# A second place for the tokens of the residual stream, with loads one tile ahead

## The chip, the cores and the metric

The kernel runs on one core of one Trainium2 chip, in one launch. The metric is the device time in microseconds (us). A core has five engines that run their own instruction streams in order and wait for one another by semaphores: TensorE (PE: matrix products and transposes), VectorE (DVE), ScalarE (ACT), GpSimd (POOL) and SyncE (SP, which issues most DMAs). ScalarE issues DMAs too, on a queue of its own. In the profile PEld is TensorE's loading of weights, which overlaps its products.

## The reference

One inference step of an encoder with one layer, over 1024 prompt tokens and 32 sample tokens (1056 in all), 1024 wide, in float32:

```
h = rmsnorm(x);  z = h @ w_in + b_in
x += w_out @ concat[ mLSTM(4 heads) | stick-breaking attention(6 heads) | S5 state space ]
x += CrossAttn(rmsnorm(x), memory K/V)    # 4 heads, 256 memory tokens
x += ConvFFN(rmsnorm(x))                  # gated, causal convolution of width 3
y  = rmsnorm(x)
```

The outputs are y, the attention's keys and values, the states of the mLSTM, of the state space and of the convolution, and the keys and values of the memory.

## The kernel before, in words

Activations lie transposed, features on the 128 partitions and tokens along the free dimension. Each float32 operand of a large product is split into a rounded part and a rest (`w_hi`, `w_lo`; `hi`, `lo`), and a product is done as three: hi x hi, hi x lo, lo x hi. Tokens are treated in three thirds of 352 (`CW`), numbered c = 0, 1, 2, or in tiles of 128 (eight prompt tiles and one of 32 sample tokens).

After the input projection three parts run side by side on all engines: the stick-breaking attention, the state space part and the mLSTM in nine chunks, in the order 0, 1, 2, 8, 3, 4, 5, 6, 7 (chunk 8 is the sample). Their results go to DRAM: `d_ya` (mLSTM), `d_yb` (attention), `d_yc` (state space). While the mLSTM goes on, the main line projects the memory's keys and values (`dense(...)` with `ev_kv`, weights `in_w_xk` and `in_w_xv`, results stored to `d_mk`, `d_mv`), and then comes the output projection `w_out(c)`. It needs the mixer outputs of third c (`y_load`) and the residual stream `xT` (zone zx) of all tokens. `ev_res` adds each product to `xT`.

`load_xT` fills `xT`: it loads a tile of tokens, [128 tokens x 1024] floats, on ScalarE's queue into a ring named "xt2", transposes it on TensorE in two halves of four transposes (`tp`), and ScalarE copies each half into `xT`. The ring has one place, at the upper end of zone zg. `Window(..., 1)` lets one tile run at a time, and `w_out` waits until `xt_done` has nine entries (line 1882).

An mLSTM chunk loads five inputs: queries (`d_qa`), keys (`d_ka`), values (`d_va`), output gates (`d_oa`) and a row broadcast `d_uu`. GpSimd adds a mask to the last, ScalarE takes four exponentials of it, one for each head, and TensorE uses them in products (`gp`). The inputs' rings have three places; `refill` (lines 1218 to 1222) gives them a fourth once the attention is done (`stick_done`).

Memory: fixed zones are dealt out by `Mem`, the first free stretch that fits, in the order of the zones; `fits(n, kind)` asks whether there is one, `Bag` holds named rings, and `grow` adds a place to a ring. The zones of float32 are named zf, zy, zx, zg in the profile, those of rounded numbers zr, za, zb, zm. A stretch that was freed is written again only once its readers are done, and those waits come from its former use.

The order of the work is fixed in two steps. All operations pass through one helper (line 173, hence "L173" in every row). A planner with a clock for each engine decides in which order the parts emit their instructions: `add` puts a part at the side, `advance` lets the parts at the side run when their clock says that they are due, `until` turns the clock on until a condition holds. A scheduler then orders each engine's stream by a timeline of its own and inserts the waits. A change of one part's memory or cost therefore moves instructions of the others.

Of the kernel before, what the change touches and what calls it, by code (L numbers as in the profile page):

```python
# [15 lines left out]
P = 128  # L16
D = 1024
KD = D // P
T = 1024
TS = 32  # L20
# [33 lines left out]
def tile_fn(tc, *args):  # L54
    nc = tc.nc
    a = dict(zip(_INS, args[: len(_INS)]))
# [120 lines left out]
    s = Timed(nc.scalar, "act")  # L177
# [51 lines left out]
    def add(x, at=None, slack=0.0):  # L229
        sd = x if isinstance(x, Window) else Side(x, chain[0], slack)  # L230
        sides.insert(len(sides) if at is None else at, sd)
        return sd
# [28 lines left out]
    with ExitStack() as top:  # L261
# [31 lines left out]
        def fits(n, kind):  # L293
            return any(m >= n for z in zones[kind] for _, m in z.heap)
# [82 lines left out]
        def rot(pool, shape, tag, bufs, dt=F32):  # L377
            x = pool.tile(shape, dt, name=tag, tag=tag)
            turn[tag] = (turn.get(tag, -1) + 1) % bufs
            alias[x.name] = f"{tag}{turn[tag]}"  # L380
            return x
# [4 lines left out]
        def tp():  # L386
            return rot(pst, [P, 4, P], "tp", 3)


        class WStream:  # L390
# [6 lines left out]
            def load(self, most=1):  # L397
                i = self.at + len(self.ready) + len(self.raw)
                if len(self.raw) > most or i >= self.end:
                    return False  # L400
                ap, kt, cols, bufs, _ = self.src[i]
                raw = bufs()[0] if bufs else rot(wpool, [P, KD, P], "w_raw", 2)
                if isinstance(ap, list):
                    g.memset(raw[:, :kt, :cols], 0.0)
                    for c0, part in ap:
                        sy.dma_start(raw[:, :kt, c0:c0 + part.shape[1]], part.rearrange("(k p) n -> p k n", p=P))
                else:
                    sy.dma_start(raw[:, :kt, :cols], ap.rearrange("(k p) n -> p k n", p=P))
                self.raw.append(raw)
                return True  # L410
# [546 lines left out]
        stick_done = []  # L957
# [793 lines left out]

        def load_xT():
            ring = Bag({"xt2": (1, D)}, top=True)

            def one(i):
                n = P if i < 8 else TS
                xt = ring.tile([P, D], "xt2")
                s.dma_start(xt[:n], a["x_prompt"][0, i * P:(i + 1) * P, :] if i < 8 else a["x_sample"][0])
                yield
                for q in range(2):  # L1760
                    ps = tp()
                    for j in range(4):
                        k = 4 * q + j
                        pe.transpose(ps[:, j, :n], xt[:n, k * P:(k + 1) * P], ident[:n, :n])
                    s.activation(xT[:, 4 * q:4 * q + 4, i * P:i * P + n], ps[:, :, :n], AF.Copy)
                    yield
                xt_done.append(i)

            w = add(Window((one(i) for i in range(9)), 1))
            while not w.done:  # L1770
                yield
            ring.free()
# [30 lines left out]
        def y_first():  # L1803
            while not (stick_done and s5_done and {0, 1, 2} <= ml_done):
                yield
            yield from y_load(0)

        add(load_xT())
        add(y_first())
        mm_mov = lambda k, c: (m_hl[:, 0, k], m_hl[:, 1, k])  # L1810
# [745 lines left out]
```

## Time and profile before

| | |
|---|---|
| median of the runs (lowest to highest, 3 runs) | 1707.65 us (1707.08 to 1707.72) |
| the profiled execution: time | 1706.09 us |
| its span, first to last instruction | 1704.3 us |
| mean granted clock of TensorE | 0.989 |
| TensorE busy | 1635.9 us, 96% |
| VectorE, ScalarE, GpSimd busy | 1132.0, 754.4, 456.8 us |
| DMA | 229.91 MB, mean 135 GB/s |

The profiled execution is one run with a time of its own; the span lies within it. Busy time is time in which an engine works on an instruction. A row of a timeline says in square brackets how long the engine was idle before it and which engine's instruction, or which DMA, ended that; the names are those of the tile written and of the tile read. The stretch in which `load_xT` runs is 466 to 642 us.

### The profile page before, as it was taken

The page shows a single profiled execution, that of the slowest core. Times are in us where ns is not written, and L with a number is a line of the kernel's source. Part 1 is how long each engine was busy: PE and PEld are TensorE (multiplying, and loading weights), DVE is VectorE, ACT ScalarE, POOL GpSimd, SP SyncE. Part 2 cuts the span into 40 slices and gives each one's busy share as a digit, 9 for nine tenths or more (in the row PEclk, how much of TensorE's full clock was granted, in tenths as well). Part 3 has the DMA queues.
Part 4 walks back from the last instruction along what each step waited for, and adds up shares of the span by engine and source line. Part 5 has one row for each costly group of instructions (what it writes and reads, how often), then busy time and mean ns, then how long its engine had stood idle before and what let it go on. Part 6 is the DMA issues. An engine that isn't in the chain of part 4 may idle for free.

```text
span 1704.3 us, 30437 instructions
## 1 busy us (share of the span) xinstructions
PE 1635.9 (96%) x11616; PEld 1593.0 (93%) x11616; DVE 1132.0 (66%) x2213; ACT 754.4 (44%) x1480; POOL 456.8 (27%) x620
## 2 busy tenths in 40 slices
PE   6999999999999989999999989999999999999997
PEld 5989989999888889999999889999999999999997
DVE  6778878835796757766656788777777777333232
ACT  6434434545565644544444553444444445111143
POOL 4234335011214322200202546533333330000022
PEclk9999999999899999999999999999999999999999
DMA  7464544254479965456554555322222227332111
GB/s 217 145 168 113 137 110 106 78 160 134 118 227 255 284 200 156 133 164 182 171 168 123 166 171 155 99 83 86 76 76 76 76 63 254 115 100 76 47 66 66
DMA packets 331592, 229.91 MB, mean 135 GB/s; under 512 B 45612, under 2 KB 312907, under 8 KB 331191
## 3 DMA queue, kind: packets, MB, share of 16 engines
q1 hardware_dynamic: 311751, 211.86, 42.5%
q10 hardware_dynamic: 19696, 16.11, 3.2%
q8 instruction: 92, 1.51, 0.4%
q14 instruction: 53, 0.43, 0.1%
HBM read 170.95 MB, written 56.38 MB: 133 GB/s over the span
## 4 chain that ended last, share of the span: by engine, by line
PE 77%; DVE 8%; DMA 7%; ACT 2%; issue 2%; POOL 2%; SPq 0%; ACTq 0%; DVEq 0%; POOLq 0%
PE mm L173 47%; PE gp L173 19%; PE tp L173 11%; DVE zy L173 3%; DVE zf L173 2%; DVE zr L173 1%; DVE zx L173 1%; POOL zy L173 1%; DMA zf<-d_act 1%; DMA out_dram<-zf 1%; POOL zf L173 1%; DVE w_lo L173 1%; ACT zf L173 1%; ACT zy L173 1%; DMA w_raw<-in_w_out_dram 1%
## 5 line engine op out<-in xcount | busy, mean ns | idle before, releaser
L173 PE MATMUL mm<-zb,w_hi 128*128 128x352 f32 (+4 forms) x1234 | 360.7, 329 | 2.9 <-ACT zb L173 1.2
L173 PE MATMUL mm<-zr,w_hi 128*128 128x352 f32 (+2 forms) x1358 | 282.2, 311 | 8.6 <-DVE zr L173 3.7
L173 PE MATMUL mm<-zb,w_lo 128*128 128x384 f32 (+4 forms) x858 | 283.6, 331 | 0.0
L173 POOL TENSOR_TENSOR zf<-zf 128x352 f32<-128x352 f32 (+5 forms) x98 | 117.5, 1200 | 579.9 <-ACT zf L173 500.5
L173 ACT ACTIVATE w_hi<-w_raw 128x1024 fp32r<-128x1024 f32 (+1 forms) x150 | 149.5, 997 | 275.0 <-PE mm L173 194.7
L173 PEld LDWEIGHTS mm<-zb,w_hi 128*128 128x128 f32 x1234 | 226.2, 190 | 4.7 <-ACT zf L173 1.3
L173 PE MATMUL mm<-zr,w_lo 128*128 128x264 f32 (+2 forms) x1026 | 225.6, 303 | 1.4 <-ACT zf L173 0.7
L173 PEld LDWEIGHTS mm<-zr,w_hi 128*128 128x128 f32 x1358 | 213.5, 189 | 10.3 <-DVE zr L173 3.9
L173 DVE TENSOR_TENSOR w_lo<-w_raw,w_hi 128x1024 fp32r<-128x1024 f32 (+1 forms) x127 | 159.9, 1259 | 60.5 <-ACT w_hi L173 59.9
L173 PE MATMUL mm<-za,w_hi 128*128 128x384 f32 (+1 forms) x552 | 184.2, 334 | 0.5 <-DVE za L173 0.5
L173 DVE TENSOR_TENSOR zx<-mm,zx 128x352 f32<-128x352 f32 (+3 forms) x120 | 62.7, 523 | 169.1 <-PE mm L173 168.7
L173 PEld LDWEIGHTS mm<-zb,w_lo 128*128 128x128 f32 x858 | 163.4, 190 | 0.7
L173 PEld LDWEIGHTS mm<-zr,w_lo 128*128 128x128 f32 x1026 | 158.6, 189 | 2.1 <-DVE w_lo L173 1.2
L173 PE MATMUL mm<-zy,w_hi 128*128 128x352 f32 x456 | 113.1, 324 | 0.0
L173 PE MATMUL tp<-ident,zf 128*128 128x128 f32 (+4 forms) x534 | 89.3, 285 | 24.6 <-DVE zf L173 21.7
L173 PE MATMUL gp<-zy 128*128 128x132 f32 (+12 forms) x698 | 105.7, 289 | 2.8 <-issue 2.1
L173 ACT ACTIVATE zf<-gp 128x512 f32<-128x512 f32 (+6 forms) x180 | 75.6, 476 | 73.6 <-PE gp L173 58.6
L173 DVE TENSOR_TENSOR zy<-zy 128x16 f32<-128x16 f32 (+9 forms) x370 | 98.5, 308 | 14.0 <-POOL zy L173 5.5
L173 PEld LDWEIGHTS mm<-za,w_hi 128*128 128x128 f32 x552 | 106.0, 192 | 1.2 <-DVE za L173 0.6
L173 POOL TENSOR_TENSOR zy<-zy 128x16 f32<-128x16 f32 (+8 forms) x123 | 83.0, 687 | 70.3 <-DVE zy L173 55.8
L173 PEld LDWEIGHTS gp<-zy 128*128 128x128 f32 (+4 forms) x698 | 93.7, 184 | 4.9 <-issue 2.9
L173 PEld LDWEIGHTS tp<-ident,zf 128*128 128x128 f32 (+4 forms) x534 | 65.0, 146 | 34.2 <-DVE zf L173 20.2
(241 smaller groups left out, 3354.3 us busy)
## 6 DMA issues: line engine op xcount, KB each, us to landing
w_raw<-in_w_ffn_a_dram SPq DMA_DIRECT2D x27, 512.0 KB
w_raw<-in_w_out_dram SPq DMA_DIRECT2D x24, 512.0 KB
w_raw<-in_w_xq_dram SPq DMA_DIRECT2D x24, 512.0 KB
w_raw<-in_w_xo_dram SPq DMA_DIRECT2D x24, 512.0 KB
w_raw<-in_w_in_dram SPq DMA_DIRECT2D x23, 512.0 KB
d_act<-zx SPq DMA_DIRECT2D x22, 528.0 KB
zf<-d_act SPq DMA_DIRECT2D x22, 528.0 KB
w_raw<-in_w_ffn_down_dram SPq DMA_DIRECT2D x16, 512.0 KB
```

The source lines that it names most:

```text
L173: return f(*args, **kw)
```

## The change

The load becomes a function of its own. It is called once at the start and again after the second half of each tile has been copied out. When a tile begins, the attention is done, the ring has one place and 1024 floats fit somewhere, the ring gets a second place and one load more is issued at once. The place is found by `Mem` as any other, here the first that fits in zone zf, and is used until all nine tiles are through.

```diff
--- before.py
+++ after.py
@@ -1751,11 +1751,24 @@
 
         def load_xT():
             ring = Bag({"xt2": (1, D)}, top=True)
+            came = []
+
+            def load():
+                i = len(came)
+                if i < 9:
+                    n = P if i < 8 else TS
+                    came.append(ring.tile([P, D], "xt2"))
+                    s.dma_start(came[i][:n], a["x_prompt"][0, i * P:(i + 1) * P, :] if i < 8 else a["x_sample"][0])
+
+            load()
 
             def one(i):
                 n = P if i < 8 else TS
-                xt = ring.tile([P, D], "xt2")
-                s.dma_start(xt[:n], a["x_prompt"][0, i * P:(i + 1) * P, :] if i < 8 else a["x_sample"][0])
+                xt = came[i]
+                if stick_done and len(ring.ring["xt2"][0]) == 1 and fits(D, "F"):
+
+                    ring.grow("xt2", D)
+                    load()
                 yield
                 for q in range(2):
                     ps = tp()
@@ -1763,6 +1776,8 @@
                         k = 4 * q + j
                         pe.transpose(ps[:, j, :n], xt[:n, k * P:(k + 1) * P], ident[:n, :n])
                     s.activation(xT[:, 4 * q:4 * q + 4, i * P:i * P + n], ps[:, :, :n], AF.Copy)
+                    if q:
+                        load()
                     yield
                 xt_done.append(i)
```

The first place at which the order changes for the argument is ScalarE around 520 us. `zf<-zf,zy` are the four exponentials of mLSTM chunk 5, `zy<-zy 32x32` those of chunk 8, `zf<-mm` and `zr<-mm` evacuate a product of the memory's keys. Before:

```order
L173 ACT_TABLE_LOAD
L173 ACTIVATE zf_87<-zf_87,zy_91 128x128 [waits Pool_49]
L173 ACTIVATE zf_87<-zf_87,zy_91 128x128 [waits DVE_49]
L173 ACTIVATE zf_87<-zf_87,zy_91 128x128 x2
L173 ACTIVATE zy_91<-zg_5311 128x96 [waits DVE_49]
L173 ACTIVATE zy_91<-zg_5311 128x96 x3
L173 ACTIVATE zx_5303<-tp_5846 128x4x128 [waits PE_49]
L173 ACTIVATE zf_87<-mm_5813 128x256 [waits DMAHW3_49,PE_49]
L173 ACTIVATE zr_83<-mm_5813 128x256 [waits DMAHW0_49]
L173 ACTIVATE zy_91<-zy_91 32x32 [waits DMAHW3_49,Activation_49,Pool_49]
L173 ACTIVATE zy_91<-zy_91 32x32 [waits Activation_49] x2
```

After:

```order
L173 ACTIVATE zf_87<-mm_5814 128x256 [waits DMAHW2_49,DVE_49,PE_49]
L173 ACTIVATE zr_83<-mm_5814 128x256 [waits DMAHW7_49]
L173 ACTIVATE zy_91<-zg_5311 128x96 [waits DVE_49]
L173 ACTIVATE zy_91<-zg_5311 128x96 x3
L173 ACTIVATE w_hi_5963<-w_raw_5812 128x1024 [waits DMAHW6_49,PE_49]
L173 ACTIVATE zf_87<-mm_5894 128x256 [waits DMAHW2_49,PE_49]
L173 ACTIVATE zr_83<-mm_5894 128x256 [waits DMAHW3_49]
L173 ACT_TABLE_LOAD [waits DMAHW1_49,Activation_49]
L173 ACTIVATE zy_91<-zy_91 32x32 [waits Pool_49]
L173 ACTIVATE zy_91<-zy_91 32x32 [waits Activation_49] x2
L173 ACTIVATE zy_91<-zy_91 32x32
```

Chunk 5's exponentials are gone from here (its `d_uu` is loaded later, into zy), and chunk 8's stand behind a further evacuation.

The second is ScalarE around 545 us in before's trace. `zf<-mm` evacuates the first product of the memory's values (mm_6024 before, mm_6057 after); `zy<-zy 128x128` are exponentials, of chunk 3 before, of chunk 4 after, and `128x96` rows are squares of a chunk's outputs. Before:

```order
L173 ACTIVATE zg_5311<-tp_6064 128x384 [waits PE_49]
L173 ACTIVATE zy_91<-zy_91 128x128 [waits DMAHW6_49,Pool_49]
L173 ACTIVATE zy_91<-zy_91 128x128 x3
L173 ACTIVATE zx_5303<-tp_6076 128x4x128 [waits PE_49]
L173 ACTIVATE zf_87<-mm_6024 128x256 [waits PE_49,Activation_49]
L173 ACTIVATE zr_83<-zf_87 128x1056 [waits DMAHW2_49]
L173 ACTIVATE zx_5303<-tp_6105 128x4x128 [waits PE_49]
L173 DMA zg_5311<-in_x_prompt_dram 128x1024 [waits DMAHW4_49,DMAHW1_49]
```

After:

```order
L173 ACTIVATE zy_91<-zy_91 32x96 [waits DVE_49]
L173 ACTIVATE zy_91<-zy_91 32x96 x3
L173 ACTIVATE zy_91<-zg_5311 128x96 [waits DVE_49,PE_49,Activation_49]
L173 ACTIVATE zy_91<-zg_5311 128x96 [waits PE_49,Activation_49] x3
L173 ACTIVATE zy_91<-zy_91 128x128 [waits DMAHW1_49,Pool_49]
L173 ACTIVATE zy_91<-zy_91 128x128 x2
L173 ACTIVATE zf_87<-mm_6057 128x256 [waits DMAHW4_49]
L173 ACTIVATE zy_91<-zy_91 128x128
L173 ACTIVATE zr_83<-tp_6113 128x256 [waits DMAHW3_49,DVE_49]
```

The evacuation stood behind chunk 3's exponentials; it now stands behind chunk 3's squares and two of chunk 4's exponentials, and the values' transposes (tp_6113) wait for it.

The third is TensorE near the end of the first third's output projection. mm_7073 is its last group, mm_7162 the first of the second third; `tp<-ident,zg 128x128` transposes the eighth tile of tokens, `tp<-ident,zf 128x32` that of the sample. Before:

```order
L173 MATMUL mm_7073<-zr_83,w_hi_7033 128x352 x2
L173 MATMUL mm_7073<-zr_83,w_lo_7034 128x352
L173 MATMUL mm_7073<-zr_83,w_hi_7033 128x352 x2
L173 MATMUL tp_6805<-ident_122,zg_5311 128x128 [waits DMAHW1_49,PE_49]
L173 MATMUL tp_6805<-ident_122,zg_5311 128x128 x3
L173 MATMUL tp_6811<-ident_122,zg_5311 128x128 [waits PE_49]
L173 MATMUL tp_6811<-ident_122,zg_5311 128x128 x3
L173 MATMUL mm_7073<-zr_83,w_lo_7034 128x352
L173 MATMUL mm_7162<-zr_83,w_hi_7067 128x352 [waits DVE_49,Activation_49]
L173 MATMUL mm_7162<-zr_83,w_hi_7067 128x352 [waits DVE_49]
L173 MATMUL mm_7162<-zr_83,w_lo_7068 128x352
```

After:

```order
L173 MATMUL mm_7039<-zr_83,w_hi_6999 128x352 x2
L173 MATMUL mm_7039<-zr_83,w_lo_7000 128x352
L173 MATMUL mm_7073<-zr_83,w_hi_7033 128x352 [waits DVE_49,Activation_49]
L173 MATMUL mm_7073<-zr_83,w_hi_7033 128x352
L173 MATMUL tp_6818<-ident_122,zf_87 128x32 [waits DMAHW0_49,PE_49]
L173 MATMUL tp_6818<-ident_122,zf_87 128x32 x3
L173 MATMUL tp_6824<-ident_122,zf_87 128x32 [waits PE_49]
L173 MATMUL tp_6824<-ident_122,zf_87 128x32 x3
L173 MATMUL mm_7073<-zr_83,w_lo_7034 128x352 [waits DVE_49]
L173 MATMUL mm_7073<-zr_83,w_hi_7033 128x352 x2
L173 MATMUL mm_7073<-zr_83,w_lo_7034 128x352
```

Before, the eighth tile's transposes stood at the end of mm_7073, and the sample's inside the next third. After, the eighth tile has been transposed before, and the sample's transposes stand at the start of mm_7073.

## Rows read from the trace of the kernel before

**Rows 1.** The page: busy us, share of the span, instructions of each engine.

```profile
PE 1635.9 (96%) x11616; PEld 1593.0 (93%) x11616; DVE 1132.0 (66%) x2213; ACT 754.4 (44%) x1480; POOL 456.8 (27%) x620
```

**Rows 2.** Windows: stretch, length, busy us (count) PE PEld DVE ACT POOL, clock, DMA share, GB/s.

```profile
500.00:520.00 20.00, 20.00 (x183) 19.88 (x182) 17.16 (x38) 12.10 (x28) 4.70 (x7) 1.00 0.96 268
520.00:540.00 20.00, 17.96 (x149) 17.49 (x148) 12.82 (x26) 12.88 (x44) 10.92 (x10) 0.91 0.82 218
540.00:560.00 20.00, 16.40 (x142) 15.17 (x141) 13.02 (x24) 10.49 (x28) 8.40 (x9) 1.00 1.05 290
...
580.00:600.00 20.00, 20.00 (x171) 19.98 (x170) 15.31 (x34) 12.85 (x43) 4.86 (x6) 1.00 0.91 273
...
620.00:640.00 20.00, 13.84 (x76) 13.11 (x75) 9.03 (x9) 8.20 (x12) 4.27 (x3) 0.83 0.90 263
640.00:660.00 20.00, 20.00 (x135) 19.92 (x134) 17.02 (x28) 11.68 (x18) 0.96 (x2) 1.00 0.61 183
```

**Rows 3.** DMA issues, 500 to 642 us: written, read, queue, count, size of one.

```profile
zg<-in_x_prompt_dram ACTq DMA_DIRECT2D x7, 512.0 KB
...
zf<-d_uu SPq DMA_DIRECT2D x1, 256.0 KB
```

**Rows 4.** Timelines of PE, ACT, POOL around 520: start, us, instruction, [idle, releaser].

```profile
525.49 0.50 PE L173 MATMUL mm<-zm,w_hi 128*128 128x256 f32 x2 [1.07 <-DVE zr L173]
...
527.08 1.75 PE L173 MATMUL tp<-ident,zg 128*128 128x128 f32 x7 [0.97 <-DVE zg L173]
...
521.62 1.28 ACT L173 ACTIVATE zf<-zf,zy 128x128 f32<-128x128 f32 x4 [2.18 <-POOL zf L173]
...
519.38 2.21 POOL L173 TENSOR_TENSOR zf<-zf,maskf 128x512 f32<-128x512 f32 x1 [4.17 <-DMA zf<-d_uu]
```

**Rows 5.** Windows, 525 to 530 us.

```profile
525.00:530.00 5.00, 3.54 (x17) 3.34 (x18) 4.85 (x10) 3.72 (x12) 1.83 (x5) 0.68 1.02 271
```

**Rows 6.** Timeline of PE, 543 to 566 us, its waits.

```profile
551.29 2.00 PE L173 MATMUL gp<-zy 128*128 128x97 f32 x16 [2.10 <-issue]
...
554.77 0.44 PE L173 MATMUL tp<-ident,zf 128*128 128x128 f32 x2 [0.81 <-ACT zf L173]
...
560.15 0.44 PE L173 MATMUL tp<-ident,zf 128*128 128x128 f32 x2 [0.84 <-ACT zf L173]
561.33 0.34 PE L173 MATMUL tp<-ident,zy 32*128 32x32 f32 x3 [0.74 <-DVE zy L173]
```

**Rows 7.** Timelines of ACT, SP and POOL, 533 to 545 us.

```profile
544.17 0.57 ACT L173 ACTIVATE zx<-tp 128x512 f32<-128x512 f32 x1
544.65 0.36 ACT L173 ACTIVATE zf<-mm 128x256 f32<-128x256 f32 x1
...
533.94 0.71 SPq L173 DMA_DIRECT2D zy<-d_uu  x1
...
543.46 0.73 SPq L173 DMA_DIRECT2D d_ya<-zy  x1
...
541.69 1.26 POOL L173 TENSOR_TENSOR zy<-zy,maskf 128x512 f32<-128x512 f32 x1 [4.37 <-DMA zy<-d_uu]
```

**Rows 8.** Timeline of PE, 628 to 643 us.

```profile
628.97 1.06 PE L173 MATMUL tp<-ident,zg 128*128 128x128 f32 x8 [1.08 <-DMA zg<-in_x_prompt_dram]
...
631.56 0.42 PE L173 MATMUL mm<-zr,w_hi 128*128 128x352 f32 x1 [1.37 <-ACT w_hi L173]
635.70 0.66 PE L173 MATMUL mm<-zr,w_hi 128*128 128x352 f32 x1 [3.71 <-DVE zr L173]
...
642.08 0.68 PE L173 MATMUL tp<-ident,zg 32*128 32x32 f32 x8
```

**Rows 9.** Chain of waits, 612 to 640 us: start, us, what.

```profile
620.57 9.78 DMA w_raw<-in_w_out_dram
```

**Rows 10.** Windows of 2 us.

```profile
624.00:626.00 2.00, 2.00 (x15) 2.00 (x14) 0.53 (x1) 0.00 (x0) 0.27 (x1) 1.00 1.10 370
...
636.00:638.00 2.00, 2.00 (x8) 2.00 (x8) 2.00 (x3) 0.50 (x1) 1.19 (x1) 0.50 0.83 239
```

## Prediction

> **What bounds the kernel now.** I read the page first, then windows of 20 us over the stretch the change can reach, then the timelines of the engines around each wait of TensorE there.
>
> On the page TensorE is busy 1635.9 us, 96% of the span [rows 1]: the time is its work plus its waits, and only what moves a wait of TensorE moves the time. Both kernels issue the same 11616 matmuls [rows 1]. Their order on TensorE is the same up to about 505 us and again from about 642 us on, so the change is worth what it shifts the moment at which TensorE has done its work up to 642 us. In that stretch the windows show TensorE full at 500 to 520 and 580 to 600, and short by 2.04, 3.60 and 6.16 us in those from 520, 540 and 620 [rows 2]. The DMA engines are near or at a full share (0.82 to 1.05) in all of these [rows 2]: a load that is moved there does not come free, it takes its bytes from another.
>
> Three places make the waits. Near 525 us TensorE waits 1.07 and 0.97 us [rows 4] and its granted clock over 525 to 530 is 0.68 [rows 5]. From 551 to 562 it waits 2.10, 0.81, 0.84 and 0.74 us, 4.49 in all [rows 6]. From 628 to 636 it waits 1.08 for the last whole tile of tokens, then 1.37 and 3.71 us for weights and mixer outputs [rows 8], and afterwards the clock is 0.50 [rows 10], the lower of the two levels (1.2 of 2.4 GHz).
>
> **The change part by part.**
>
> The loads. Nine loads stay nine: eight of 512 KB [rows 3] and one of 128 KB. They stand on ScalarE's queue. With a second place, the fifth is issued as soon as the attention has left, and each later one about a tile ahead. Only one of the loads is waited for before: the eighth, 1.08 us [rows 8]. That is all a load made earlier can give by itself, and it is hidden in part, because behind it TensorE waits for weights anyway.
>
> What the second place takes away. It is the first that fits, in zone zf, where before the fourth place of the mLSTM's inputs began. So chunk 5's values, output gates and weights (its uu) move from zf to zy, whose places come free later, and the two loads of the cached memory keys (256 KB each) wait until the tokens of the sample have left the place: they go from the stretch after 580 us to the burst after 620 us. This is the larger part of the change.
>
> 1. The wait near 525 us. Before, the mask addition of chunk 5 ran on GpSimd at 519.38, after a wait of 4.17 us for uu, and ScalarE, which works in order, stood 2.18 us for it; behind it stood the evacuation that TensorE needed [rows 4]. After, chunk 5's exponentials are no longer there (first piece of order), so the 1.07 and most of the 0.97 go. The clock: 0.68 of full over 5 us [rows 5] is a loss of 0.32 x 3.54 busy us = 1.1 us. I take 1.07 + 0.8 + 1.1 = 3.0 us saved; bounds 0 (chunk 8's exponentials, which wait for GpSimd too, stand near and take the place) and 3.2.
>
> 2. The middle, 540 to 565 us. The evacuation of the first values (zf<-mm, at 544.65 before [rows 7]) stood behind chunk 3's exponentials. After, it stands behind two of chunk 4's (second piece of order), and the transposes of these values hold up everything behind them on TensorE. When can chunk 4's exponentials run? Its uu is issued right behind the store d_ya of chunk 2 (543.46 before [rows 7]), which after stands behind chunk 3's exponentials on ScalarE: an estimate is 545. A load of uu (256 KB [rows 3]) took from 533.94 to 541.69 = 7.75 us here [rows 7], the addition of the mask 1.26 us [rows 7]: 545 + 7.75 + 1.26 = 554.0, plus two exponentials and the evacuation, about 0.6 + 0.4: 555. TensorE reached the same count of instructions before some 1.2 us ahead of the wait that ended at 551.29, so at 551.29 - 2.10 - 1.2 = 548.0. That makes it 7 us later than before there. Against it the four old waits behind that place, 4.49 us [rows 6], can go, since their data has had time. A wait of this length brings the lower clock behind it: after the 3.71 us wait the rows show a window of 2 us at 0.50 [rows 10], half of full, at which 2 us do the work of 1; I take 2 us for it. 7 - 4.5 + 2 = 4.5 us lost. Bounds: 0 (uu issued 4 us earlier, or the load faster in a calmer stretch) and 9 (the old waits stay). The value taken lies by the one row that shows a load of uu in this stretch.
>
> 3. The end, 620 to 640 us. SP's order there is the same: the reloads of the projected memory and the weights for the first group of the second third (w_raw), which spent 9.78 us from issue to landing [rows 9]. While they run, the queues move 370 GB/s [rows 10]. In that burst 128 KB of sample tokens now stand in place of 512 KB: 384 KB less, 393,216 bytes / 370 GB/s = 1.1 us earlier. The chain from there to 635.70 (round the weights, split the mixer output, subtract) is as long as before, but for two copies of the sample's tokens now on ScalarE inside it, an estimated 0.2 us each, from the 0.57 us of the same copy with four times as many columns [rows 7]: +0.4. The eight transposes of the sample, 0.68 us [rows 8], come ahead of the wait (third piece of order), under it, and no longer behind: -0.7. Together -1.4. The 1.08 us wait for the tile is gone, but only lengthens the wait behind it. Bounds: -4 (the wait shrinks so far that the clock stays up) and +1.2 (the sample's tokens, 128 KB behind two reloads on ScalarE's queue, land as late as the eighth tile did, at 628.97, and the rest of their group of matmuls runs only then). The cached keys' 512 KB now follow in this burst, ahead of a weight that is needed one group later; at 370 GB/s they are 1.4 us, and TensorE has no wait from 640 to 660, so I cost them at nothing; without that cover 1.4.
>
> The Trainium skill (DMA: Bandwidth & Descriptors, section "Queues, rings and completion order") says that each DMA engine takes turns between the queues that have work, a packet at a time. By that rule bytes taken from ScalarE's queue speed SP's only while ScalarE's is empty; it still holds four reloads, so the 1.1 us would be near 0 and the end -0.3. The row of 9.78 us bears out the sharing; which bytes shared it, no row here shows.
>
> Sum: -3.0 + 4.5 - 1.4 = +0.1 us on the profiled execution's 1706.09 us: 1706.2. The median of the runs shown is 1707.65, 1.56 higher, so 1707.8.
>
> **The rivals.**
>
> A, faster: chunk 4's exponentials are not late. The middle then costs 0 to 1, steps 1 and 3 remain: -3.0 + 0.5 - 1.4 = -3.9, with the end at its better bound -6.5: 1701 to 1704. For it: the old waits of this stretch hung on loads that go out in another order now, the store of chunk 2 can move ahead with the 3 us of step 1, and TensorE, were it to wait, would leave the DMA engines time. Against it: the DMA share of 1.05 [rows 2], at which a load of 256 KB took 7.75 us.
>
> B, slower: one mechanism, chunk 4's uu. It decides from the point at which it lands later than about 553 us. If it lands at 556 (its issue before was about 5 us behind the store of chunk 2; 543.46 + 5 + 7.75), and the mask is added by 557.5, TensorE is 10 us late at the values' transposes; 10 - 4.5 + 2 = +7.5, less 1.5 to 3 of step 1 and the 1.4: +3.1 to +4.6, to +8 if the old waits stay: 1711 to 1716.
>
> C, the loads were hidden anyway and the moved chunk loads find as much room in zy: every wait of before stays but the 1.08 and the end's 1.4: -1.4, 1706.2, within no change. Nothing in the order speaks for waits staying word for word, so it has a small part of that case.
>
> **How the numbers follow.** A measurement of this kernel tells 0.2%, 3.4 us, from no change. Forecast with C: 0.37. A: 0.32. B: 0.31. Only the upper part of the forecast's own spread (about 1704.5 to 1711) reaches over the bound, and the upper end of A falls within it, which about cancel: faster 0.31, within 0.38, slower 0.31. As both signs hold most of the chance, the likeliest case's own range is 1704.5 to 1711; the range for 8 in 10 reaches into A and B: 1700.5 to 1715.
>
> **What would show it.** Step 1: no wait of TensorE of over 0.5 us and a full clock from 520 to 530. Step 2: one wait of TensorE of 5 us or more between 543 and 558, released by ScalarE's zf, with ScalarE idle for GpSimd's mask addition just before; if there is none, A. Step 3: no wait for tokens of 1 us, and the wait that ended at 635.70 ending 1 to 2 us earlier relative to the store of the last chunk. The prediction is wrong if a wait appears outside 505 to 645 us, or if the windows from 520 to 600 are full.

## The result: slower by 0.6%, and the profile after

The changed kernel takes 1714.32 us in the median of 9 runs (1713.67 to 1724.77), the kernel before 1707.72 us in runs beside it. The medians are 6.6 us apart; the ratio, taken over all runs, is 1.0059, with a 95% interval of 1.0041 to 1.0077: 7 to 13 us slower. The forecast was no change; the time lies at the upper end of the stated range, in rival B. The profiled execution takes 1713.83 us, its span is 1712.0 us.

Where the time went shows at two landmarks that both orders share: the first product of the memory's keys, ahead of the reordered stretch, and the first product of the residual stream's norm, behind it. TensorE's timeline of before:

```profile
476.29 0.50 PE L173 MATMUL mm<-zm,w_hi 128*128 128x256 f32 x2 [0.50 <-DMA zm<-d_mT]
...
641.48 0.67 PE L173 MATMUL gp<-ones,zf 128*128 128x1 f32 x6
```

and of after:

```profile
476.83 0.51 PE L173 MATMUL mm<-zm,w_hi 128*128 128x256 f32 x2 [0.48 <-DMA zm<-d_mT]
...
651.20 0.67 PE L173 MATMUL gp<-ones,zf 128*128 128x1 f32 x6
```

The stretch takes 165.2 us before and 174.4 after, 9.2 more. The span grew by 7.7: 0.5 us was lost ahead of the stretch and 2.0 came back behind it. The time behind it is no effect to read from one execution: over the traces of the kernels here it lies anywhere from 1060.8 to 1069.9 us.

The windows of 20 us of after (columns as in [rows 2]) place the loss:

```profile
520.00:540.00 20.00, 19.46 (x173) 18.61 (x172) 16.14 (x35) 14.12 (x41) 7.60 (x9) 1.00 0.90 248
540.00:560.00 20.00, 12.98 (x75) 11.78 (x74) 12.49 (x23) 6.24 (x25) 6.95 (x9) 0.66 1.08 288
560.00:580.00 20.00, 18.39 (x143) 18.15 (x143) 12.09 (x23) 11.69 (x32) 6.83 (x5) 0.83 0.71 184
```

520 to 540 is nearly full and at full clock now, where before 2.04 us were idle and the clock was 0.91 [rows 2, 5]. 540 to 560 has 75 products instead of 142 [rows 2]. Its windows of 5 us, and those behind it:

```profile
545.00:550.00 5.00, 3.83 (x20) 3.28 (x20) 4.42 (x10) 3.27 (x9) 0.83 (x1) 0.64 1.08 320
550.00:555.00 5.00, 5.00 (x27) 5.00 (x27) 2.61 (x6) 0.70 (x5) 1.56 (x3) 0.50 1.12 289
555.00:560.00 5.00, 1.00 (x5) 0.70 (x4) 4.31 (x8) 1.34 (x10) 2.45 (x3) 0.50 1.18 275
560.00:565.00 5.00, 3.40 (x17) 3.40 (x18) 1.74 (x5) 4.05 (x15) 2.31 (x2) 0.50 0.87 203
565.00:570.00 5.00, 5.00 (x37) 5.00 (x37) 3.20 (x4) 3.40 (x10) 1.91 (x1) 0.81 0.64 179
```

The clock is at or near its lower level for some 20 us. Busy time times the share of the clock that is missing gives 1.38 + 2.5 + 0.5 + 1.7 + 0.95 = 7.0 us lost by clock alone. The waits of TensorE after, where [rows 4, 6 and 8] have those of before:

```profile
546.17 0.46 PE L173 MATMUL tp<-ident,zf 128*128 128x128 f32 x2 [3.01 <-ACT zy L173]
...
561.61 0.69 PE L173 MATMUL tp<-ident,zf 128*128 128x128 f32 x2 [5.61 <-ACT zf L173]
...
587.01 0.52 PE L173 MATMUL tp<-ident,zg 128*128 128x128 f32 x3 [1.21 <-DVE zg L173]
...
595.99 0.55 PE L173 MATMUL tp<-ident,zy 96*128 96x96 f32 x4 [1.92 <-ACT zg L173]
...
606.99 0.59 PE L173 MATMUL mm<-zr,w_hi 128*128 128x352 f32 x2 [0.96 <-ACT zf L173]
...
640.29 0.65 PE L173 MATMUL tp<-ident,zf 32*128 32x32 f32 x8 [3.54 <-DMA zf<-in_x_sample_dram]
...
647.08 0.43 PE L173 MATMUL mm<-zr,w_hi 128*128 128x352 f32 x1 [0.71 <-DVE zr L173]
```

Two waits of 3.01 and 5.61 us stand where four of 4.49 in all stood. Both are ScalarE's. The timelines there of GpSimd, ScalarE and, last, VectorE:

```profile
542.77 1.27 POOL L173 TENSOR_TENSOR zy<-zy,maskf 128x512 f32<-128x512 f32 x1 [6.36 <-DMA zy<-d_uu]
...
556.73 1.25 POOL L173 TENSOR_TENSOR zy<-zy,maskf 128x512 f32<-128x512 f32 x1
...
544.08 1.27 ACT L173 ACTIVATE zy<-zy 128x128 f32<-128x128 f32 x4 [4.71 <-POOL zy L173]
...
545.26 0.85 ACT L173 ACTIVATE zy<-tp,vecC 128x128 f32<-128x128 f32 x3
...
554.30 0.28 ACT L173 ACTIVATE zy<-zy 32x96 f32<-32x96 f32 x1 [6.03 <-DVE zy L173]
...
559.11 0.28 ACT L173 ACTIVATE zy<-zg 128x96 f32<-128x96 f32 x1 [3.64 <-DVE zg L173]
...
560.32 0.97 ACT L173 ACTIVATE zy<-zy 128x128 f32<-128x128 f32 x3
561.19 0.36 ACT L173 ACTIVATE zf<-mm 128x256 f32<-128x256 f32 x1
...
556.01 2.99 DVE L173 TENSOR_TENSOR zg<-zg,zy 128x384 f32<-128x384 f32 x2
```

In ScalarE's timeline of before, chunk 2's copies ran ahead of chunk 3's exponentials:

```profile
538.32 0.86 ACT L173 ACTIVATE zy<-tp,vecC 128x128 f32<-128x128 f32 x3
...
542.99 1.28 ACT L173 ACTIVATE zy<-zy 128x128 f32<-128x128 f32 x4 [3.42 <-POOL zy L173]
```

Read after's rows from the top: chunk 3's uu lands at 542.7, its mask is added, its exponentials run at 544.08 after ScalarE has stood 4.71 us, and behind them the three copies of chunk 2's outputs, which hold a transpose buffer that TensorE waits for until 546.17. Now the clock is low, chunk 3's products run at half speed, its outputs are late on VectorE, and ScalarE stands 6.03 and 3.64 us for the squares of chunk 8 and chunk 3. The evacuation of the first values, at 561.19, comes behind them, and with it TensorE. Chunk 4's mask was added by 558.0, before chunk 3's squares: its uu was not the last to come. Without chunk 3's squares the evacuation could have stood at about 559.0 (an estimate: 558.0 and the 0.97 us of three exponentials), so that some 2.2 us of the 5.61 are chunk 3's alone. Half speed is not all of chunk 3's lateness: the first of the two VectorE additions at 556.01 took 2.4 us, where the other took 0.6. GpSimd's power and chunk 4's mask addition ran at that time; whether they slowed it, no run here tests.

### The profile page after: what moved, and what is told of

Same layout as the page of the kernel before. It is cut to its first block, busy times and chain, and to the rows that moved or that the text cites. A ratio compares the mean times of both kernels' runs of the same rounds, so it can differ in the third digit from the quotient of the medians.

```text
span 1712.0 us, 30432 instructions
## 1 busy us (share of the span) xinstructions
PE 1638.6 (96%) x11616; PEld 1596.1 (93%) x11616; DVE 1135.3 (66%) x2213; ACT 753.9 (44%) x1480; POOL 452.6 (26%) x620
## 4 chain that ended last, share of the span: by engine, by line
PE 76%; DVE 9%; DMA 7%; ACT 3%; issue 2%; POOL 1%; SPq 0%; ACTq 0%; DVEq 0%; POOLq 0%
PE mm L173 46%; PE gp L173 19%; PE tp L173 11%; DVE zy L173 3%; DVE zf L173 2%; DVE zx L173 1%; ACT zy L173 1%; DVE zr L173 1%; DVE w_lo L173 1%; DMA zf<-d_e 1%; DMA zf<-d_act 1%; ACT zf L173 1%; DMA w_raw<-in_w_in_dram 1%; DMA out_dram<-zf 1%; SPq L173 0%
## 5 line engine op out<-in xcount | busy, mean ns | idle before, releaser
L173 PEld LDWEIGHTS gp<-zy 128*128 128x128 f32 (+5 forms) x706 | 97.2, 189 | 2.5 <-ACT zf L173 0.9
```

Of the source, the lines that this page charges most:

```text
L173: return f(*args, **kw)
```

## The experiments

Each was timed in five rounds against the kernel before on the same chip. The ratio is to that kernel, with its 95% interval; a ratio of 0.001 is 1.7 us.

| run | what it is | median us | ratio |
|---|---|---|---|
| (after) | the change | 1714.32 | 1.0059 [1.0041, 1.0077] |
| disp | before, the place in zf taken and not used | 1706.85 | 1.0008 [0.9989, 1.0027] |
| one | the change without the second place | 1714.43 | 1.0050 [1.0033, 1.0068] |
| late | the second place taken after the mLSTM's | 1718.34 | 1.0075 [1.0054, 1.0096] |
| two | second place, loads issued at a tile's start | 1708.89 | 0.9999 [0.9983, 1.0015] |
| evdve_after | the values' evacuation on VectorE | 1717.21 | 1.0067 [1.0047, 1.0087] |
| y2dve | chunk 2's output copies on VectorE | 1716.64 | 1.0061 [1.0038, 1.0083] |
| ydve | all chunks' output copies on VectorE | 1708.83 | 1.0013 [1.0001, 1.0026] |
| ydve_before | the same in before | 1708.03 | 1.0011 [0.9997, 1.0025] |
| ydve_one | the same in one | 1712.87 | 1.0035 [1.0020, 1.0051] |
| ydve_two | the same in two | 1706.24 | 0.9997 [0.9980, 1.0013] |
| c3s1 | chunk 3 one step later | 1717.85 | 1.0060 [1.0044, 1.0077] |
| c3s2 | chunk 3 two steps later | 1720.39 | 1.0077 [1.0058, 1.0095] |
| qk1 | chunks 3 to 7 a step later inside | 1718.67 | 1.0081 [1.0052, 1.0109] |
| first | the change, its first load where before had it | 1707.09 | 1.0008 [0.9994, 1.0022] |
| first_ah | the same, later loads not counted by the planner | 1707.12 | 1.0007 [0.9992, 1.0022] |
| two_early | two, its first load ahead of the tile | 1715.84 | 1.0052 [1.0033, 1.0071] |

**The place in memory, and the loads.** Two runs part the change: disp takes the place and moves no load, one moves the loads and takes no place.

```diff
 # disp (before)
+                if stick_done and not held_place and fits(D, "F"):
+                    held_place.append(Mem(D))
 # one (after)
-                if stick_done and len(ring.ring["xt2"][0]) == 1 and fits(D, "F"):
-                    ring.grow("xt2", D)
-                    load()
```

> The kernel before, which takes the second place in zf at the same moment and leaves it unused: loads as before, but chunk 5's values, gates and uu go to zy and come later. Theory M (the place's displacement of chunk 5 is what slows the changed kernel, by crowding the DMA of 540 to 565 us): slower than before by 4 us or more, 1711 to 1716, with a wait of 3 us or more between 540 and 562. Theory O (the order is what slows it: the evacuation of the first values stands on ScalarE behind chunk 3's squares and chunk 4's exponentials; here it stands right behind chunk 3's exponentials, as before): 1703 to 1708, no wait of over 3 us in that stretch; the wait near 525 us gone.

> The changed kernel without the second place: the load of a tile is only issued at the end of the one before instead of at its own start. Chunk 5 stays in zf. TensorE's order of chunks 0 to 3 is that of the changed kernel, and the values' evacuation stands behind the squares of chunk 8 alone. Theory M: as before, 1705 to 1709. Theory O: within 1705 to 1710, as the evacuation waits for nothing of chunk 3's outputs or chunk 4; if chunk 3's early place on TensorE alone is the fault, 1711 or more with a wait of 3 us at its first products.

disp is as fast as before, though it moves chunk 5 to zy as the change does. It has a wait of over 3 us, which theory O had excluded, and half speed behind it (16 products of this shape took 2.00 us in before [rows 6]):

```profile
549.10 3.67 PE L173 MATMUL gp<-zy 128*128 128x97 f32 x16 [3.44 <-issue]
```

But from 480 to 660 us TensorE loses no more than in before: 18.3 us against 18.9, where after loses 28.0 (idle time, and busy time times the missing share of the clock, from windows of 20 us).

one is as slow as the change, with one place: theory M falls. Of theory O only the time of its last clause came true, over 1711. The wait of 3.07 us at 552 stands at the memory's transposes, released by ScalarE, not at chunk 3's first products, and a longer one of 4.12 us stands at 523. In late (the same line with a flag that the mLSTM sets once its rings have grown) the place is in zy, and chunk 5 stays:

> The changed kernel, whose second place is taken only after the mLSTM's fourth places have been: it comes from zy, chunk 5 stays in zf, loads run ahead from the fifth tile on. The values' evacuation stands behind one square of chunk 3. Theory M: 1702 to 1708, faster than the changed kernel by 6 us or more. Theory O: between the two, 1707 to 1713, with a wait for that evacuation of 2 to 5 us. Theory X (the tokens' loads ahead of time crowd the DMA): as the changed kernel, 1712 to 1718.

It is slow too, though no chunk was moved: M is out, and O, which set 2 to 5 us for the evacuation (1.98 was seen), does not explain its 1.0075. In two the place and the loads ahead are as in the change, but a load is issued in the first step of a tile:

```diff
             def one(i):
+                if len(came) == i:
+                    load()
                 xt = came[i]
...
                     ring.grow("xt2", D)
+                if len(ring.ring["xt2"][0]) == 2 and len(came) == i + 1:
                     load()
...
-                    if q:
-                        load()
```

> The second place in zf and loads one tile ahead as in the change, but a tile's load is issued at the start of a tile (as before), not at the end of the one before. ScalarE and TensorE keep the order of the kernel before around chunks 2 to 4. Theory P (what slows the changed kernel is that the early issue makes the planner put chunk 3 ahead: its exponentials ahead of chunk 2's output copies on ScalarE, its products ahead of the values' group on TensorE): as before or a little faster, 1702 to 1708, no wait of over 3.6 us before 620. Theory X (loads ahead of time crowd the DMA): 1710 or more.

0.9999: a second place with loads one tile ahead costs nothing and gives nothing that the interval of 0.0016 to either side would show. Theory X falls too.

**Single waits taken away.** evdve_after puts the first copy of the values' evacuation on VectorE (`v.tensor_copy` for `s.activation`), y2dve the three output copies of chunk 2, ydve those of all chunks:

```diff
 # ydve; y2dve the same with "if c == 2"
-                    s.activation(yt[:, j, :n], yps[:, j, :n], AF.Copy, scale=va("gn_a", j))
+                    v.tensor_scalar(yt[:, j, :n], yps[:, j, :n], va("gn_a", j), None, op0=ALU.mult)
```

> The changed kernel with the first copy of each evacuation of the memory's values on VectorE instead of ScalarE, so that it no longer stands in ScalarE's order behind chunk 3's squares and chunk 4's exponentials. Theory O: the wait of 5.6 us and the half clock around it go, 1706 to 1711. Theory M: the chain of chunk 3 and 4 is late whatever stands behind it, the wait moves to another place, 1712 to 1717.

> The changed kernel with the output copies of chunk 2 alone on VectorE; ScalarE's order around it stays that of the changed kernel, and the evacuation of the first values stands behind chunk 3's squares as there. Theory P: TensorE's wait of 3.0 us for the transpose buffer near 546 goes and the clock does not fall before chunk 3's products; the wait for the values' evacuation (5.6 us) stays, in whole or shorter, as chunk 3 runs at full clock: 1707 to 1712. If the chain from chunk 3's uu sets the time, the wait moves to chunk 3's products and the kernel stays at 1712 to 1718.

> The changed kernel with the copies of the mLSTM's outputs (three for a chunk) on VectorE instead of ScalarE. TensorE's wait for a transpose buffer that chunk 2's copies hold behind chunk 3's exponentials (3.0 us) must go. Theory P: 1707 to 1712. If the chain from chunk 3's uu alone sets the time, as slow as the changed kernel, 1712 to 1717.

evdve_after and y2dve keep the changed kernel's order, and stay slow: the first misses theory O's range, the second theory P's and lies in that of the chain from chunk 3's uu. TensorE's waits in evdve_after, then in y2dve:

```profile
545.27 0.69 PE L173 MATMUL tp<-ident,zf 128*128 128x128 f32 x2 [3.80 <-ACT zy L173]
...
559.01 0.69 PE L173 MATMUL tp<-ident,zf 128*128 128x128 f32 x2 [3.84 <-DVE zf L173]
```

```profile
547.03 0.55 PE L173 MATMUL tp<-ident,zy 96*128 96x96 f32 x4 [2.23 <-ACT zy L173]
...
559.35 0.69 PE L173 MATMUL tp<-ident,zf 128*128 128x128 f32 x2 [3.63 <-ACT zf L173]
```

The evacuation waits in VectorE's queue now (DVE zf), and with chunk 2's copies gone, the next transposes wait for ScalarE (ACT zy) in their stead. Taking one waiter out of a queue lets the next one take its place. ydve recovers most, but its order changed as a whole. Its controls:

> The kernel before, with the copies of the mLSTM's outputs on VectorE. There they stood ahead of the next exponentials on ScalarE, so that no transpose waits for them. Theory P (the copies cost time only where they stand behind exponentials): as before, 1704 to 1709. Theory G (VectorE is the better place for them in general): 1698 to 1704.

> The changed kernel without the second place (loads issued at the end of the tile before), with the copies of the mLSTM's outputs on VectorE. Theory P: the waits of 4.1 us at 523 and 3.1 us at 552 shrink, 1704 to 1711, at least 4 us under the same kernel with the copies on ScalarE. If not, 1712 to 1717.

> Loads one tile ahead, issued at a tile's start, second place in zf, and the copies of the mLSTM's outputs on VectorE. Theory P: as the same kernel with the copies on ScalarE, 1704 to 1709. Theory G: 1696 to 1703, faster than both kernels.

Where the order is that of before (ydve_before, ydve_two), the copies' engine makes no difference of over 0.25%: theory G falls. In one they give back 0.15%, 2.6 us, where theory P wanted at least 4: 1712.87 lies in the range set for P being wrong, and as the two intervals overlap, not even the 0.15% is sure. What else slows one stands on GpSimd and TensorE around 520:

```profile
519.95 1.26 POOL L173 TENSOR_TENSOR zf<-zf,maskf 128x512 f32<-128x512 f32 x1 [3.63 <-DMA zf<-d_uu]
521.17 2.62 POOL L173 TENSOR_TENSOR zy<-zy,mhalf 128x4 f32<-128x4 f32 x2
...
522.93 0.87 PE L173 MATMUL tp<-ident,zy 128*128 128x128 f32 x3 [4.12 <-DVE zy L173]
```

Here chunk 5's mask addition waits for its uu ahead of chunk 0's power (mhalf), and TensorE waits 4.12 us for chunk 0's outputs. Before, that power came first, at 512.90:

```profile
512.90 1.02 POOL L173 TENSOR_TENSOR zy<-zy,mhalf 128x4 f32<-128x4 f32 x1 [0.38 <-DVE zy L173]
...
519.38 2.21 POOL L173 TENSOR_TENSOR zf<-zf,maskf 128x512 f32<-128x512 f32 x1 [4.17 <-DMA zf<-d_uu]
```

It is the same trap at an earlier chunk: the start of a later chunk, which waits for its load, ahead of the end of an earlier one, in the queue of an engine that works in order. In the changed kernel chunk 5 has been moved away, and chunk 3 does it to chunk 2.

**Chunk 3 held back.** c3s1 and c3s2 give chunk 3 one and two empty steps at its start, qk1 gives chunks 3 to 7 one before their key transposes:

```diff
+                for _ in range(1 if c == 3 else 0):      # c3s2: 2; qk1: if 3 <= c <= 7
+                    yield
```

> The changed kernel, with mLSTM chunk 3 started one step of the planner later. Chunk 2's output copies stand ahead of chunk 3's exponentials on ScalarE again, and the first two evacuations of the values ahead of chunk 3's squares; chunk 3's products keep their place on TensorE, and the second place falls into zy. Theory P: the two waits of 3.0 and 5.6 us shrink to under 4 us in all, 1706 to 1712. Theory C (chunk 3's products stand too early on TensorE, whatever ScalarE's order is): 1711 to 1718, a wait of 3 us or more at their place.

> As the run before, with chunk 3 started two steps later: its products stand 46 instructions later on TensorE than in the changed kernel. Theories P and C: 1703 to 1709, waits of under 4.5 us in all from 540 to 565 and no half clock there. If it stays at 1712 or more, neither ScalarE's order nor chunk 3's place is the cause.

> The changed kernel with one step of the planner more before the key transposes of chunks 3 to 7. On ScalarE chunk 2's output copies stand ahead of chunk 3's exponentials, and the first two evacuations of the values ahead of chunk 3's squares and chunk 4's exponentials; on TensorE chunk 3's products stand where the changed kernel has them, ahead of the values' next group. Theory P (ScalarE's order decides): no wait of over 2.5 us from 540 to 565, 1704 to 1710. Theory C (TensorE's order decides, as nothing is left in front of chunk 3's products to cover the wait for its uu): a wait of 3 us or more at or just before chunk 3's products, and half clock behind it, 1711 to 1718.

All three stay slow, outside theory P's ranges, and c3s2 is outside C's too: by its own terms neither theory holds as it was put. In c3s1 and c3s2 chunk 2's copies did run ahead of chunk 3's exponentials (550.67 before 555.37, 543.99 before 548.95), so that this one trap is not what a slow kernel needs; both have the trap of one instead, waits of 3.16 and 2.94 us for VectorE at 527.80 and 520.94. In c3s2 chunk 4 overtakes chunk 3 in the state, which changes the mLSTM's values but not its work. Its longest wait is another one, for a store that holds the evacuation's place (TensorE, then ScalarE):

```profile
559.96 0.69 PE L173 MATMUL tp<-ident,zf 128*128 128x128 f32 x2 [10.87 <-ACT zf L173]
...
559.52 0.68 ACT L173 ACTIVATE zf<-mm 128x256 f32<-128x256 f32 x2 [4.95 <-DMA out_dram<-zf]
```

qk1 was to tell ScalarE's order from TensorE's. It did not: two of chunk 2's three copies stood behind chunk 3's exponentials still, and TensorE waited 3.42 us for them, then 5.98 elsewhere:

```profile
542.69 1.11 PE L173 MATMUL tp<-ident,zf 128*128 128x128 f32 x4 [3.42 <-ACT zy L173]
...
580.84 0.79 PE L173 MATMUL mm<-zm,w_hi 128*128 128x256 f32 x2 [5.98 <-ACT zf L173]
```

**One line.** What do one, late and the change share that two does not? The first load stands ahead of the first tile. The planner holds a part back by the latency of what its last step issued. Issued outside the tile, the load's latency is not counted to it, and the first transposes are due at once. They run 10.6 us earlier, in before and then after:

```profile
505.81 0.60 PE L173 MATMUL tp<-ident,zg 128*128 128x128 f32 x4
```

```profile
495.22 0.60 PE L173 MATMUL tp<-ident,zg 128*128 128x128 f32 x4
```

They wait for nothing there; but all that the planner places behind them is placed anew. The load itself is issued at the same point on ScalarE, in before and then after:

```profile
466.33 0.37 ACTq L173 DMA_DIRECT2D zg<-in_x_prompt_dram  x1
```

```profile
467.30 0.37 ACTq L173 DMA_DIRECT2D zg<-in_x_prompt_dram  x1
```

So it is not the load's traffic that moved, but what is ordered by it. In all eleven kernels with that line ahead of the first tile the first transposes run at 492 to 501 us, in the seven without it at 504 to 510. That line alone was then moved, out of the change (first, first_ah) and into two (two_early):

```diff
 # first (after); two_early adds the first load() to two
-            load()
-
             def one(i):
+                if i == 0:
+                    load()
 # first_ah: besides
                     if q:
-                        load()
+                        ahead(load)
```

> The changed kernel, whose first load alone is issued inside the first tile's first step, as before, and no longer ahead of it. All other loads and the second place are as in the change. Theory F (the planner counts a load's latency only in the step that issues it; a load issued ahead of the first tile lets the first transposes count as due at once, and the whole order behind them turns): the first transposes go back behind 500 us, chunk 3's products 14 instructions back on TensorE, 1703 to 1710. Theory X (the loads at the end of a tile are at fault): 1712 to 1718.

> As the run before, and the later loads are issued without their latency being counted to the tile's own clock in the planner. TensorE and ScalarE have the order of the kernel before around chunks 2 to 4. Theory F: 1702 to 1709. Theory X: 1712 to 1718.

> The kernel with loads ahead that was as fast as before (each load at a tile's start), whose first load alone is now issued ahead of the first tile, as in the change. Theory F: the slow order comes back, 1711 to 1718, with a wait of 3 us or more near 523 or near 550. Theory X: 1703 to 1710.

The change without its early first load is at 1.0008 and 1.0007, and the fast kernel with it at 1.0052. In two_early the trap of one is back on TensorE:

```profile
521.15 0.87 PE L173 MATMUL tp<-ident,zy 128*128 128x128 f32 x3 [3.52 <-DVE zy L173]
```

So the cause is shown by undoing it and by doing it alone: the place of the first load in the code. That it acts by way of the order is read from the traces. Which waits the early order makes differs from kernel to kernel: in two_early chunk 2's copies run ahead of chunk 3's exponentials (543.83 before 548.37), and its longest wait is the trap at 521; and ydve, with the early line, loses little. In sum the kernels at 1.0013 or below lose 15.9 to 19.7 us of TensorE from 480 to 660 us, those at 1.0035 or above 23.1 to 30.8. None of the kernels beats the one before by more than its interval.

## Why the prediction was wrong, step by step

The steps of the sum, in lost time of TensorE (idle plus clock), from the rows above and those of before:

| step | forecast | measured |
|---|---|---|
| 1, near 525 us | -3.0 | -2.7: 3.14 us before, 0.46 after |
| 2, 540 to 570 us | +4.5 (0 to 9) | +11.1: 4.49 before, 3.01 + 5.61 + 7.0 after |
| between, 575 to 611 us | 0 | +1.9: 2.16 before (1.49 at 578.46, 0.67 at 610.92), 4.09 after |
| 3, 620 to 650 us | -1.4 (-4 to +1.2) | -2.6: 6.16 + 2.35 before, 4.25 + 1.7 after |
| sum | +0.1 | +7.8 (before rounding) |

Between the landmarks it was 9.2; another 1.1 us is lost at 480 to 500, where after's window has a clock of 0.96 and the order is the same up to 495.

Step 1 was right: chunk 5's exponentials were gone, and the stall and the low clock with them. Step 3 lies in its range, by luck in part: the wait for the sample's tokens, named as its bad bound, came true (3.54 us, where "no wait for tokens of 1 us" was to show the step), and in exchange the waits for weights and mixer outputs behind it fell from 5.08 to 0.71 us. The sentence from the Trainium skill (DMA: Bandwidth & Descriptors, section "Queues, rings and completion order") on queues that take turns decided nothing here: the sizes of the end by the one and by the other were 1.1 us apart, and the measured end was better than both.

Step 2 is the one that failed: it is "the middle, 540 to 565 us", and it was mis-sized by 6.6 us and rested on an incomplete cause. The place was right (the values' evacuation, ScalarE behind chunk 3 and 4, a wait of over 5 us). But the wait was put down to chunk 4's uu alone. That was later than forecast (its mask added by 558.0, against 554.0), and three of its exponentials stand ahead of the evacuation, not two; still, ScalarE waited last for chunk 3's outputs. They were late because a first wait, for the copies behind chunk 3's exponentials, had already brought the clock down: 16 of chunk 3's products took 3.57 us against 2.00 before [rows 6]; VectorE's slow addition came on top. That first wait was not seen, though the step names the order that made it: it has chunk 2's store behind chunk 3's exponentials, and draws from it only that chunk 4's uu comes later, not that TensorE waits for the transpose buffer that these copies empty. And the clock was priced at 2 us, from one wait of 3.71 us followed by matmuls that were all ready [rows 8, 10]; here two waits, with little but chunk 3's products between them, left it low for some 20 us and cost 7.0. The stretch from 575 to 611 us was put at nothing without a reason, and lost 1.9.

Rival B, slower by chunk 4's uu, has the direction, the price (1711 to 1716) and the mask's time (557.5, against 558.0), but only part of the cause, so that its time came out partly by luck: it has neither the first wait nor the clock's 7.0 us. Rival C's claim that the loads were hidden holds: two and first show it. What the prediction lacked was the question which part of the code turned the order. The sign was in TensorE's order, which it calls the same up to about 505 us: the first tile's transposes had moved from 505.81 to 495.22. It took the second place's displacement for "the larger part of the change"; disp puts it at 0.0008, and at 0.0027 at the upper end of its interval, and the line that did it was not mentioned.

What stays open: whether ScalarE's order or TensorE's is the worse half of the trap, as qk1 did not part them; why c3s1, c3s2 and qk1 stay slow after the moves that theory P asked for; and what made VectorE's addition slow.

## What to carry to other kernels

Where a planner sets the order, a line that moves a load can cost more by what it does to the planner's due times than the load is worth; test it with kernels that do only that, before the wait that shows in the trace is repaired. In queues that work in order, look for the start of a later piece, which waits for a load, ahead of the end of an earlier piece that the main engine needs; taking one waiter out of such a queue only shows the next. Do not price the clock behind a wait from one row: it cost about 2 us behind the wait of 3.71 us here, and 7.0 around two waits that followed each other.

## What was not expected of the hardware

The half clock lasted through 550 to 555 us, a window in which TensorE was busy all 5.00 us, most of them 16 products of chunk 3 that took 3.57 us, against 2.00 in before [rows 6]:

```profile
549.38 3.57 PE L173 MATMUL gp<-zy 128*128 128x97 f32 x16
```

In two, which is as fast as before, the same 16 products took 3.70 us behind a wait of 2.47:

```profile
553.93 3.70 PE L173 MATMUL gp<-zy 128*128 128x97 f32 x16 [2.47 <-issue]
```

Before, behind the wait that ended at 635.70, the window from 640 on is at full clock again [rows 2, 8].
